# Two token groups' even projections by seven block products, attention's division moved to the gates, and its streams reordered

## The chip, the cores and the metric

One core of a Trainium2 chip runs the whole kernel. The metric is the device time of one execution in microseconds. TensorE (PE) multiplies, VectorE (DVE), ScalarE (ACT) and GpSimd (POOL) work on tiles, and all DMA is issued from the queue of SyncE (SP).

## The reference

Two sequences (2048 and 512 tokens, width 1024) go through two layers with the same weights. All is float32.

```python
def even_sublayer(x, w_in, ...):
    u = x @ w_in
    qa, ka, va, za, gd, qb, kb, vb, zb = jnp.split(u, _offsets(EVEN_SPLITS), axis=-1)
    ya = gla_mixer(qa, ka, va, za, gd, ...)   # gated linear attention, both directions, 4 heads
    yb = swa_mixer(qb, kb, vb, zb, rel_bias, sink)   # |i-j| <= 128, softmax with a sink, 8 heads
    return jnp.concatenate([ya, yb], axis=-1) @ w_out
...
    e = jnp.exp(s - m)
    p = e / (jnp.sum(e, -1, keepdims=True) + jnp.exp(sk - m))
    o = jnp.einsum('bnkgqs,bnskd->bnqkgd', p.astype(v.dtype), vb).reshape(Bn, L, SWA_WIDTH)
    return o * jax.nn.silu(z)
```

The odd layer is a projection to 4096, a gated convolution of width 3 and an output projection. Each layer ends in a LayerNorm of a residual sum.

## The kernel before

The 2560 tokens form five groups of 512: groups 0 to 3 are the long sequence, group 4 is the short one. A float32 factor is split into a high and a low part of TensorE's fp32r type, and a product of two factors is three passes (high by high, high by low, low by high), each a matmul of 128 x 128 by 512 columns.

The even input projection of a group has two kinds of stage. `tok` (`e1_tok`, L1025) makes what is wanted with tokens on partitions, in 336-wide products. `ch` (`e1_ch`, L1071) makes 21 tiles of 128 channels: for each, `dense_ch` (L569) runs 24 products into one PSUM bank, eight slices of the inner dimension by three passes. Tiles 0 to 3 are the keys, 4 to 7 the queries of the linear attention, 8 the keys and 9 to 12 the queries of the softmax attention, 13 to 16 and 17 to 20 their gates. Between them `decay` runs the small matmuls that make the decays.

Attention is cut in 20 chunks of 128 tokens. `gla_stream` (L1454) goes through a chunk with `inside` (L1186): seven levels of pairwise decay products on VectorE, each with small matmuls of 32 or 64 columns, and at its end the transposes and the state update; then `along` (L1402) goes forward. `swa_front` (L1510) makes scores, exponentials and their sums (`den`) and divides the tile `P` by them; `swa_back` (L1579) turns `P` by transposes, splits it and multiplies by the values; at the end it multiplies by the gate (`gb`) and stores to `mix_s`.

The order on the engines is written by a planner in the kernel. `Model` keeps a clock for each engine; dense stages run as the main thread, and `Flow.pump` (L337) steps side streams, by rank, whenever TensorE's clock passes the time at which their inputs are due. Attention is thus laid between the dense products. `Flow.until` (L346) runs side streams alone when a dense stage needs a mark that isn't there yet. Weights arrive by `fetch`, are split by ScalarE (`cook`, tile `wh`) and GpSimd (`cook_low`, tile `wl`).

In the odd layer two pairs of groups (`odd_pair`, L1944) already multiply 2 x 2 blocks with seven products of half the inner dimension: activations' differences from `prep_pair` (L909), weights' differences and splits from `pair_weights` (L1858), and VectorE sums that put the products together. A unit is seven products of 12 matmuls.

All recorded instructions have line L242, since one helper issues them; tiles tell them apart. `acc` and `ps` are PSUM banks (four each), `st` the activations' parts, `wh` and `wl` the weights' parts, `md`, `pr` and `y` working tiles; names ending in `_s` lie in HBM.

The stages stand in this order (`run`, L2103): tok4 ch4 tok3 ch3 tok2 ch2 tok1 ch1 oe4 tok0 ch0 one4 oe0 oo4 oe1 oe2 pair0 oe3 oo0 pair1 oo1 oo2 oo3, where oe and oo are output projections of the even and the odd layer and one4 is the odd layer's projection of group 4.

Of the kernel before, what the change touches and what calls it, by code (L numbers as in the profile page):

```python
# [262 lines left out]
class Flow:  # L263
# [32 lines left out]
    def flush(self, everything=False, name=None):  # L296
        now, keep = [], []
        for one in self.late:
            (now if everything or name in one[2] or (name is None and one[0] <= self.t) else keep).append(one)
        self.late = self.model.late = keep  # L300
        for one in now:
            one[1]()
# [74 lines left out]
class Trunk:  # L377
    def __init__(self, tc, nc, I, y_out, ctx):
# [23 lines left out]
        self.vb_s = dr("vb_s", (NC, 128, 256))  # L402
        self.qf_s = dr("qf_s", (NC, 128, 512))
# [10 lines left out]
        self.blocks = []  # L414
# [154 lines left out]
    def dense_ch(self, xh, xl, w=None, last=True):  # L569
# [3 lines left out]
        p = self.pd()  # L573
# [13 lines left out]
        if last:  # L587
            self.drop(wl)
        return p
# [86 lines left out]
    def setup(self):  # L676
# [9 lines left out]
        self.dtot = c.tile([128, NC, 4], F32, name="dtot")  # L686
# [47 lines left out]
    def setup_bias(self):  # L734
        nc, I, c = self.nc, self.I, self.const
        yield from self.setup_late()
        oh = self.e((32, 512), "gb", bufs=2)
        nc.sync.dma_start(oh[:], I["onehot"])
        ml = self.e((8, 512), "gb", bufs=2)
# [6 lines left out]
        line = self.e((8, 512), "pth", bufs=2)  # L746
# [4 lines left out]
        for h in range(8):  # L751
            rows = self.e((128, 512), "ptl", bufs=2)
# [5 lines left out]
        yield 6.0  # L758
        self.bias = [self.new(self.e2, (128, 4, 385), F32, "P", 4, True) for _ in range(2)]
# [35 lines left out]
    def prep(self, key, src, gates, homes=None, then=None, fix=None, deep=1, each=None):  # L795
# [10 lines left out]
        eager, homes = homes is not None, homes or self.half  # L806
# [218 lines left out]
    def e1_tok(self, g):  # L1025
# [9 lines left out]
        stores = {"gla_in": 24, "swa_in": 29, "done_sw": 33, "done_e1_": 37}  # L1035
# [35 lines left out]
    def e1_ch(self, groups, us):  # L1071
# [3 lines left out]
        if us[0] == 0:  # L1075
            if groups == (4,):
# [25 lines left out]
        def split(g, u, p):  # L1102
            sc = 1.0 if u == 8 else 0.125
            hi, lo = self.m2(dt=F32R), self.m2(dt=F32R)
# [6 lines left out]
            def store():  # L1111
                for i, o in enumerate((hi, lo)):
                    for hh in range(2):
# [4 lines left out]
                        else:  # L1118
                            nc.sync.dma_start(
                                self.qb_s[4 * g:4 * g + 4, 64 * i:64 * i + 64, 2 * (u - 9) + hh].rearrange("c p t -> p c t"),  # L1120
                                s.rearrange("p (c t) -> p c t", c=4))
                self.left[g]("swa_in")
            flow.defer(rest, hi, lo, p)

        def take(g, u, p):
            if u < 8:
# [7 lines left out]
                if u == 0:  # L1134
# [3 lines left out]
                    X = G[g] = self.new(self.yp, (128, 512), F32R, "y", 4, True)  # L1138
# [12 lines left out]
            if 1 < u < 10:  # L1151
                decay(g, (u - 2) // 4, (u - 2) % 4)

        for u in us:
# [7 lines left out]
            if u == 9:  # L1162
                self.drop(up, *(G[g] for g in groups))
                up = self.up = None
                G.clear()
        if u == 16:
            for g in groups:
                self.release("e1_%d" % g)
                flow.mark("end_e1_%d" % g)

# [8 lines left out]

    def gla_load_k(self, c):  # L1180
        K = self.e((128, 2, 512), "KK")
# [1023 lines left out]
```

## Time and profile before

| | us |
|---|---|
| median of three runs | 2368.6 (2367.55 to 2372.68) |
| profiled execution | 2370.12 |
| its span, first to last instruction | 2368.1 |
| TensorE busy | 2343.9 |
| VectorE busy | 1582.8 |
| GpSimd busy | 1418.4 |
| ScalarE busy | 1226.1 |

The profile has a page and views that group the same instructions: by engine and tile, by stretch of time, by waits, by DMA issue. TensorE's matmuls overlap, so the mean length of one is more than the time from one start to the next; the count in a stretch gives the pace. Softmax attention runs from 162.1 us (its first reciprocal of `den`) to 1261.1 us (the last store of `gb`).

### The profile page before, as it was taken

What the parts mean: (1) busy time and instruction counts of PE and PEld (TensorE: products, weight loads), DVE (VectorE), ACT (ScalarE), POOL (GpSimd) and SP (SyncE); (2) the same over time, 40 slices, a digit from 0 to 9 for tenths busy, and PEclk for the clock granted to TensorE, in tenths of its full rate; (3) what the DMA queues carried; (4) which work ended last, traced back from release to release, by engine and by line L of the source; (5) the groups of instructions that cost most, each with busy time, mean ns of one, the idle gap of its engine ahead of it and who ended that gap; (6) DMA issues with size and microseconds to landing.
All of it is one profiled execution on the core that took longest, in us unless ns stands there. A gap on an engine that the chain in (4) does not pass through costs nothing.

```text
span 2368.1 us, 43087 instructions
## 1 busy us (share of the span) xinstructions
PE 2343.9 (99%) x15830; PEld 1951.8 (82%) x15830; DVE 1582.8 (67%) x2699; ACT 1226.1 (52%) x2363; POOL 1418.4 (60%) x1610
## 2 busy tenths in 40 slices
PE   8999999999999999999999999999999999999998
PEld 8888889888988888888888888878888877888887
DVE  2267756767767677577776467876566587656567
ACT  4666776656576645665577532543334343333431
POOL 5454435443444444444444467898887689988674
PEclk9999999999999999999999999999999999999999
DMA  7977686676667657675478777232124633221573
GB/s 230 295 226 233 221 269 229 209 221 221 218 194 236 223 173 242 197 218 161 158 245 268 266 261 243 92 116 89 52 78 140 217 105 103 73 72 58 175 242 121
DMA packets 275057, 437.37 MB, mean 185 GB/s; under 512 B 21360, under 2 KB 160240, under 8 KB 274848
## 3 DMA queue, kind: packets, MB, share of 16 engines
q1 hardware_dynamic: 274848, 434.64, 56.5%
q8 instruction: 125, 2.05, 0.4%
q14 instruction: 84, 0.69, 0.1%
HBM read 319.72 MB, written 114.84 MB: 184 GB/s over the span
## 4 chain that ended last, share of the span: by engine, by line
PE 87%; DVE 5%; POOL 4%; DMA 2%; issue 1%; ACT 1%; SPq 0%; POOLq 0%; DVEq 0%; ACTq 0%
PE acc L242 71%; PE ps L242 17%; POOL wl L242 1%; POOL wh L242 1%; DVE st L242 1%; DVE bst L242 1%; DVE y L242 1%; POOL md L242 0%; SPq L242 0%; DVE QQ L242 0%; DVE P L242 0%; DVE KK L242 0%; DMA K<-kb_s 0%; DMA mix_s<-gb 0%; DMA op_s<-QQ 0%
## 5 line engine op out<-in xcount | busy, mean ns | idle before, releaser
L242 POOL TENSOR_TENSOR wl<-ws,wh 128x256 fp32r<-128x256 f32 (+1 forms) x912 | 750.7, 855 | 711.4 <-PE acc L242 478.0
L242 PE MATMUL acc<-st,wh 128*128 128x512 f32 x3160 | 828.5, 395 | 2.8 <-DVE pr L242 2.0
L242 PEld LDWEIGHTS acc<-st,wh 128*128 128x128 f32 x3160 | 580.9, 188 | 121.0 <-issue 3.1
L242 PE MATMUL acc<-st,wl 128*128 128x512 f32 x1744 | 471.9, 395 | 2.8 <-POOL wl L242 1.9
L242 PE MATMUL acc<-wh,st 128*128 128x512 f32 (+1 forms) x1680 | 389.4, 371 | 7.9 <-ACT st L242 6.4
L242 PEld LDWEIGHTS acc<-st,wl 128*128 128x128 f32 x1744 | 320.8, 188 | 68.0 <-POOL wl L242 4.1
L242 PEld LDWEIGHTS acc<-wh,st 128*128 128x128 f32 x1680 | 300.2, 189 | 55.1 <-ACT st L242 6.4
L242 ACT CAST wh<-ws 128x1024 fp32r<-128x1024 f32 (+2 forms) x252 | 249.0, 989 | 184.2 <-DMA ws<-in_w_oo 55.9
L242 PE MATMUL acc<-wl,st 128*128 128x512 f32 (+1 forms) x840 | 209.0, 368 | 0.6 <-POOL wl L242 0.5
L242 ACT ACTIVATE md<-md 128x512 f32<-128x512 f32 x264 | 164.7, 631 | 20.5 <-DVE md L242 14.9
L242 PEld LDWEIGHTS acc<-wl,st 128*128 128x128 f32 x840 | 150.7, 188 | 23.8 <-POOL wl L242 1.3
L242 DVE SCALAR_TENSOR_TENSOR md<-acc,md 128x512 f32<-128x512 f32 (+1 forms) x113 | 77.0, 683 | 81.5 <-ACT md L242 76.5
L242 DVE TENSOR_TENSOR st<-pr,st 128x512 fp32r<-128x512 f32 x115 | 98.5, 874 | 41.6 <-ACT st L242 41.2
L242 ACT ACTIVATE md<-acc 128x512 f32<-128x512 f32 (+1 forms) x133 | 76.2, 597 | 67.0 <-PE acc L242 66.5
L242 POOL TENSOR_TENSOR wh<-md,wh 128x256 fp32r<-128x256 f32 x118 | 96.7, 842 | 13.6 <-ACT wh L242 13.1
L242 ACT CAST pth<-ps 128x512 fp32r<-128x512 f32 x112 | 65.3, 583 | 73.1 <-PE ps L242 72.3
L242 DVE CUSTOM_DVE_ANT_0 P<-ps,P 128x384 f32<-128x384 f32 (+1 forms) x160 | 79.3, 525 | 29.6 <-PE ps L242 29.0
L242 ACT ACTIVATE P<-P,nm 128x385 f32<-128x385 f32 (+1 forms) x160 | 93.2, 587 | 3.9 <-DVE nm L242 3.9
L242 ACT ACTIVATE mv<-mv,eps 128x1 f32<-128x1 f32 x40 | 11.8, 295 | 151.8 <-DVE mv L242 147.7
L242 PE MATMUL acc<-P,wh 128*128 128x512 f32 x312 | 89.5, 400 | 0.4 <-POOL wh L242 0.4
L242 ACT COPY km<-KK 128x512 f32<-128x512 f32 x80 | 50.8, 635 | 72.2 <-DVE KK L242 50.9
L242 ACT CAST st<-pr 128x512 fp32r<-128x512 f32 x115 | 68.3, 617 | 30.3 <-DMA pr<-mix_s 12.9
(490 smaller groups left out, 4090.2 us busy)
## 6 DMA issues: line engine op xcount, KB each, us to landing
ws<-in_w_ch SPq DMA_DIRECT2D x105, 512.0 KB, 4.4
ws<-in_w_od SPq DMA_DIRECT2D x58, 512.0 KB, 4.2
ws<-in_w_oe SPq DMA_DIRECT2D x40, 512.0 KB, 3.8
ws<-in_w_oo SPq DMA_DIRECT2D x36, 512.0 KB, 3.5
K<-kb_s SPq DMA_DIRECT2D x32, 384.0 KB, 6.3
d_s<-md SPq DMA_DIRECT2D x40, 256.0 KB, 4.2
qb_s<-md SPq DMA_DIRECT2D x80, 128.0 KB, 3.9
tA<-d_s SPq DMA_DIRECT2D x20, 512.0 KB, 5.7
```

Of the source, the lines that this page charges most:

```text
L242: r = f(*a, **k)
```

## The change

**Even pair.** Groups 4 and 3 are projected together. The stages become tok4, tok3, one `ch` stage for both in which tile 0 is done plainly for each group, and then ten units (`even_pair`, new) of two channel tiles each by seven products of half the inner dimension. `prep_even` (new) makes the activations' differences on VectorE from the parts `st` that lie on chip, and puts their splits in the tiles that attention uses later (P, Q, K0, K1, V, pth, ptl, gb). `pair_weights` now serves these units too and writes two of its sums in place. Softmax attention's bias tiles are loaded after the units, when P is free.

```diff
+        even = [(1, 2), (3, 4), (5, 6), (7, 8), (13, 14), (15, 16), (9, 10), (11, 12), (17, 18), (19, 20)]
-        stages = [("tok", 4), ("ch", ((4,), A + B)), ("tok", 3), ("ch", ((3,), A + B)),
+        stages = [("tok", 4), ("tok", 3), ("ch", ((4, 3), [0], even)),
...
+        for k in range(4):
...
+            b11, b12, b21, b22 = raws
+            t = self.take(places, (128, 512))
+            sub(t[:], b12[:], b11[:])
+            sub(b12[:], b22[:], b12[:])
+            sub(b22[:], b22[:], t[:])
+            sub(b21[:], b21[:], b22[:])
...
+            for i in (1, 6, 7, 5, 2, 4, 3) if n else (1, 2, 6, 7, 5, 4, 3):
+                if n == 0 and i in (4, 5, 6, 7):
+                    yield "paire_%d" % i
...
+                p = u[i] = self.pd(hold=True)
+                for k in range(4):
+                    c = slice(k * 128, k * 128 + 128)
+                    nc.tensor.matmul(p[:], w[:, 0, c], H[i][k], start=(k == 0), stop=False)
+                    nc.tensor.matmul(p[:], w[:, 0, c], L[i][k], start=False, stop=False)
+                    yield
+                for k in range(4):
+                    c = slice(k * 128, k * 128 + 128)
+                    nc.tensor.matmul(p[:], w[:, 1, c], H[i][k], start=False, stop=(k == 3))
...
+        for i in (6, 7, 5):
+            yield "free_paire_%d" % i
```

**Division at the gates.** The four divisions of a half-block's P on VectorE go. The reciprocals are stored to a new HBM array `rd_s`, element by element, read back once per chunk as rows repeated over 64 partitions, and multiplied into the gate on GpSimd.

```diff
-                for h in range(4):
-                    nc.vector.tensor_scalar(Pt[:, h, :w], Pt[:, h, :w], den[:, h:h + 1], None, op0=ALU.mult)
...
+                    nc.sync.dma_start(self.rd_s[c, kv].rearrange("h t -> t h"), den[:])
+                    if kv:
+                        self.flow.mark("rd_%d" % c, max(0.0, self.model.clock["sync"] - self.flow.t) + 10.0)
...
+                            nc.sync.dma_start(rb[64 * i:64 * i + 64], bass.AP(a.tensor, a.offset + (2 * c + i) * 512, [[0, 64], [1, 512]]))
...
+            nc.gpsimd.tensor_tensor(flat, flat, rb[:], op=ALU.mult)
```

**Streams.** `inside` ends after its seven levels; what followed is `behind`, run by a stream of its own, `gla_behind`, gated by a mark per chunk, while `gla_stream` starts the next chunk (two chunks open at most). Level 2 now copies Q apart, as level 8 did. In `swa_back` the transposes of the next block are issued before the split of the last is done, where a PSUM bank is free. Softmax attention's streams move from rank 2 to rank 1. `flush` runs each deferred step once even if a step runs others.

```diff
+    def gla_behind(self):
+        nxt = []
+        for c in [*range(19, 15, -1), *range(15, -1, -1)]:
+            yield "head_%d" % c
...
-        flow.add(self.swa_front())
-        flow.add(self.swa_back())
+        flow.add(self.gla_behind(), rank=1)
+        flow.add(self.swa_front(), rank=1)
+        flow.add(self.swa_back(), rank=1)
```

How the instructions move, at three places. TensorE before, in the channel stage of group 4: each tile is 16 passes by `wh` and 8 by `wl`, and the first small products of linear attention (tiles `qn`, `QQ`, `KK`) stand between them.

```order
L242 MATMUL acc<-st,wh 128x512 x16
L242 MATMUL acc<-st,wl 128x512 x8
L242 MATMUL acc<-st,wh 128x512 x14
L242 MATMUL ps<-qn,KK 32x32 x16
L242 MATMUL ps<-QQ,KK 32x32 x16
L242 MATMUL acc<-st,wh 128x512 x2
```

TensorE in the change, inside a unit: two products of 12 on `st` alone and on the differences in P, Q and gb, with a level of linear attention between.

```order
L242 MATMUL acc<-st,wh 128x512 x12
L242 MATMUL ps<-md,km 32x32 x16
L242 MATMUL ps<-QQ,km 32x32 x16
L242 MATMUL acc<-st,wl 128x512 x12
L242 MATMUL acc<-P,wh 128x512 x4
L242 MATMUL acc<-Q,wh 128x512 x2
L242 MATMUL acc<-gb,wh 128x512 x2
```

What moved: a tile pair takes 84 products for two groups instead of 96, and attention's small products now stand in the units. Next, VectorE in softmax attention before: the reciprocal is followed by four divisions, ahead of a gate's step (`md`) and a level of linear attention.

```order
L242 TENSOR_TENSOR ptl<-ps,pth 128x512
L242 RECIPROCAL den<-den 128x4
L242 TENSOR_SCALAR P<-P,den 128x384 x4
L242 SCALAR_TENSOR_TENSOR md<-acc,md 128x512
L242 TENSOR_TENSOR QQ<-QQ,tC 128x64x2x4
```

In the change the next step follows the reciprocal at once, and splits of two turned blocks (`ptl`) stand together.

```order
L242 TENSOR_TENSOR ptl<-ps,pth 128x512 x2
L242 RECIPROCAL den<-den 128x4
L242 TENSOR_TENSOR gb<-ps,gb 64x512
L242 TENSOR_TENSOR ptl<-ps,pth 128x512 x2
L242 ISA P,mx<-ps,P 128x384
```

What moved: the divisions left VectorE's queue. SP before, where softmax attention loads its gate (`gb`) among the weight tiles and the stores of the projections:

```order
L242 DMA mix_s<-gb 512x1x128
L242 DMA gb<-gb_s 128x512
L242 DMA ws<-in_w_ch 128x1024
L242 DMA qb_s<-md 64x4x128 x4
L242 DMA qf_s<-QQ 128x512
```

SP in the change, around the second read-back: other transfers, the read-back in two halves, the write of the next half-block's reciprocals, and the next weight tile behind them.

```order
L242 DMA vb_s<-md 128x256
L242 DMA pr<-in_xT 128x512
L242 DMA md<-rd_s 64x512 x2
L242 DMA k_s<-md 128x4x128
L242 DMA rd_s<-den 128x4x1
L242 DMA ws<-in_w_ch 128x1024
```

What moved: the `rd_s` rows are new, and weight tiles stand behind them; SP has 1304 DMA issues before and 1360 now.

More of the change, by code (lines that the diff above doesn't have):

```diff
@@ L296, in flush @@
     def flush(self, everything=False, name=None):
[L297 to L300, printed above, removed]
+        now = [one for one in self.late if everything or name in one[2] or (name is None and one[0] <= self.t)]
         for one in now:
-            one[1]()
+            if any(one is x for x in self.late):
+                self.late[:] = [x for x in self.late if x is not one]
+                one[1]()
     def force(self, *tiles):
@@ L793, in let_go, with prep @@
                 self.drop(t)
-    def prep(self, key, src, gates, homes=None, then=None, fix=None, deep=1, each=None):
+    def prep(self, key, src, gates, homes=None, then=None, fix=None, deep=1, each=None, wide=False):
         nc = self.nc
@@ L804, in prep @@
         raws = []
-        eager, homes = homes is not None, homes or self.half
+        eager, homes = homes is not None, homes or self.half + (self.mids if wide else [])
         todo = list(range(8))
@@ L1161, in e1_ch @@
                 yield
-            if u == 9:
+            if u == 7 and not units:
                 self.drop(up, *(G[g] for g in groups))
@@ L1165, in e1_ch @@
                 G.clear()
+        if units:
+            own = self.owned["e1_%d" % groups[1]]
+            self.drop(*own[:2])
+            del own[:2]
+            flow.mark("plain_e")
+            yield from self.even_pair(groups, units, take, put, decay)
         if u == 16:
@@ L1178, in gla_load, with gla_home @@
         return q, T1
+    def gla_home(self, tag):
+        done = self.flow.done
+        rows = "swa_in1" in done and "res_x1_4_3" not in done
+        return [(self.e2, tag, 1)] if rows or self.model.spare(tag, 1) else self.large[:1]
     def gla_load_k(self, c):
-        K = self.e((128, 2, 512), "KK")
+        K = self.take(self.gla_home("KK"), (128, 2, 512))
         for i in range(2):
@@ L1232, in inside @@
         base = None
-        Sb = self.bst if not last else None
         wait = []
@@ L1452, in seq, with ahead @@
         return (0, 16) if g < 4 else (16, 20)
+    def gla_behind(self):
+        nxt = []
+        for c in [*range(19, 15, -1), *range(15, -1, -1)]:
+            yield "head_%d" % c
+            v = nxt.pop() if nxt else self.load_v(c)
+            def ahead():
+                if c not in (0, 16) and "gla_in%d" % ((c - 1) // 4) in self.flow.done:
+                    nxt.append(self.load_v(c - 1))
+            yield from self.behind(*self.heads.pop(0), v, ahead)
+            v = None
     def gla_stream(self):
+        nxt = {}
```

424 lines of the change are left out of this document (332 added, 92 removed).

## The prediction

> **What bounds the kernel now.** I read the spans first, then the page's busy shares, the chain that ended last, what TensorE waited for, and then stretches of the run, because the run has two kinds of work.
>
> ```profile
> core 0: 2368.1 us, clock 0.998
> PE 2343.9 (99%) x15830; PEld 1951.8 (82%) x15830; DVE 1582.8 (67%) x2699; ACT 1226.1 (52%) x2363; POOL 1418.4 (60%) x1610
> PE 87%; DVE 5%; POOL 4%; DMA 2%; issue 1%; ACT 1%; SPq 0%; POOLq 0%; DVEq 0%; ACTq 0%
> L242 PEld LDWEIGHTS acc<-st,wh 128*128 128x128 f32 x3160 | 580.9, 188 | 121.0 <-issue 3.1
> ```
>
> The clock is full (0.998), TensorE is busy for 99% of the span, and 87% of the chain is TensorE's own time. A busy TensorE may still be one that starts products slowly, so I looked at stretches. The columns are the stretch, its length, then busy time and instructions of TensorE, weight loads, VectorE, ScalarE, GpSimd, then clock, DMA share and GB/s.
>
> ```profile
> 59.20:118.40 59.20, 59.20 (x263) 49.03 (x262) 12.48 (x18) 36.20 (x56) 27.43 (x39) 1.00 0.97 295
> 473.60:532.80 59.20, 59.20 (x634) 48.51 (x633) 40.74 (x82) 34.42 (x62) 26.88 (x30) 1.00 0.75 221
> 1065.60:1124.80 59.20, 58.89 (x560) 47.88 (x559) 47.01 (x102) 35.38 (x70) 27.28 (x31) 1.00 0.51 161
> 1480.00:1539.20 59.20, 58.27 (x278) 47.54 (x277) 49.84 (x64) 31.00 (x57) 48.70 (x46) 1.00 0.29 92
> 1539.20:1598.40 59.20, 57.13 (x242) 46.06 (x241) 45.22 (x54) 23.91 (x38) 57.23 (x55) 0.97 0.33 116
> 1657.60:1716.80 59.20, 59.20 (x260) 48.52 (x259) 34.15 (x43) 23.30 (x33) 48.22 (x50) 1.00 0.15 52
> 1894.40:1953.60 59.20, 57.20 (x263) 46.17 (x262) 52.72 (x65) 26.13 (x50) 51.92 (x48) 1.00 0.31 105
> 1953.60:2012.80 59.20, 57.64 (x250) 46.55 (x250) 45.29 (x51) 23.61 (x39) 55.67 (x54) 1.00 0.30 103
> ```
>
> The stretch from 1657.6 holds nothing but 512-wide products: 260 in 59.20 us, one every 0.2277 us. That is my price of a dense product. From 59.2 to 118.4, where group 4 runs its channel projections alone, TensorE goes at the same pace, with VectorE only 21% busy. In the stretches with attention between the dense products (473.6, 1065.6) TensorE still has next to no idle time. The idle time that there is lies at the starts of the two seven-product stages of the odd layer.
>
> ```profile
> PE acc L242 <- ACT st L242: 6.4, 1, 6.4
> PE acc L242 <- POOL wl L242: 2.4, 3, 1.1
> PE acc L242 <- DVE pr L242: 2.0, 2, 1.3
> ```
>
> In the table of TensorE's waits (us in total, times, longest) the largest is the one at the program's start. So the run is as long as TensorE's list of work, and a shorter list shortens it unless a new wait fills the hole.
>
> By the Trainium skill's page "Perfetto Trace Analysis", section "Identifying the Most-Contended Engine", matmul busy time is a poor measure of headroom and the busy share of weight loads is a better one; here that share is 82%, which would leave 18%. By that rule the removed work would be 120 weight loads of 0.188 us (the last row above), an estimate of 22.6 us instead of the 27.3 below. The trace speaks for the product count: in the stretch from 1657.6, which cannot go faster, the weight loads are also at 48.52 of 59.20 us, 82%.
>
> **Seven products for eight.** Twenty of 21 channel tiles of groups 4 and 3 go from 10 x 2 x 2 x 24 = 960 products to 10 x 7 x 12 = 840; every other kind of TensorE instruction keeps its count. All are 512 wide, so the list is 120 x 0.2277 = 27.3 us shorter. The weight pieces change too: 40 tiles of 1024 columns become 70 of 512.
>
> ```profile
> L242 POOL TENSOR_TENSOR wl<-ws,wh 128x256 fp32r<-128x256 f32 x852 | 712.2, 868 | 677.2 <-PE acc L242 467.0 <-ACT wh L242 137.9 <-PE ps L242 12.4
> L242 POOL TENSOR_TENSOR md<-ws,md 128x512 f32<-128x512 f32 x9 | 11.7, 1297 | 0.0
> L242 DVE TENSOR_TENSOR md<-acc,md 128x512 f32<-128x512 f32 x91 | 61.1, 681 | 13.4 <-PE acc L242 11.3 <-ACT md L242 1.3
> L242 DVE TENSOR_TENSOR st<-pr,st 128x512 fp32r<-128x512 f32 x115 | 98.5, 874 | 41.6 <-ACT st L242 41.2
> ```
>
> (After the count: busy us, mean ns of one, then idle time before and what ended it.) A unit of seven products lasts 84 x 0.2277 = 19.1 us. GpSimd makes 14 low halves of 0.868 us in it, 12.2 us, and up to four weight sums of 1.297 us, 5.2 us: 17.4 us in all, under the 19.1. In the stretch from 1657.6 it carries 48.22 of 59.20 us in the same pattern with no idle TensorE, so I cost it at nothing; if that cover failed, each us over 19.1 would cost ten, one per unit. The DMA load halves per unit of time (two tiles per 19.1 us instead of one per 24 x 0.2277 = 5.5 us).
>
> VectorE adds 7 sums of 0.681 us per unit, 4.8 us. The differences of the activations are 48 instructions of 128x512 between 0.681 and 0.874 us, 33 to 42 us in all, and most of them fall in the first 70 us, where the stretch from 59.2 shows that VectorE has room. But the last must be done before the first unit's third product. The nearest rows are the starts of the odd pairs, where parts are also made and products wait for them: 0.93 + 2.07 us of idle TensorE and a clock of 0.97 from 1480 to 1598, and 2.00 + 1.56 us from 1894 to 2013, so 3.6 to about 4.8 us (the 0.03 of clock is 1.8 us). The added start could be hidden (0) or be both of these in a row (8.4). I take 6, since the tok part of group 3 now runs in the same 30 us and needs VectorE for its own results.
>
> The clock belongs to that price:
>
> ```profile
> 1549.60 0.73 PE L242 MATMUL acc<-st,wl 128*128 128x512 f32 x2 [1.14 <-POOL wl L242]
> 1551.27 1.08 PE L242 MATMUL acc<-st,wl 128*128 128x512 f32 x2 [0.94 <-DVE acc L242]
> ```
>
> Two waits of 1.14 and 0.94 us stand 1.7 us apart in the one odd-layer stretch whose clock fell to 0.97, so waits of this size bunched at a start may cost nearly twice their length. The Trainium skill's page "TensorE: Matmul & The Clock Gate", section "The HAM clock gate", has the clock halve only after an idle window of about 3.4 us; the trace does not agree, as no wait in that stretch is that long.
>
> **Attention in less time.** The softmax attention can start only when the units are done, since its tiles hold the differences: counted over the order with the prices of the trace, some 275 us into TensorE's list instead of some 140. Both kinds of attention still end in the first part of oe0. Softmax attention so has some 17% less time; linear attention starts as early as before. VectorE loses the divisions.
>
> ```profile
> L242 DVE TENSOR_SCALAR P<-P,den 128x384 f32<-128x384 f32 x128 | 61.6, 543 | 1.1
> L242 DVE TENSOR_SCALAR P<-P,den 128x256 f32<-128x256 f32 x32 | 10.9, 405 | 0.3
> L242 POOL TENSOR_TENSOR gb<-gb 128x512 f32<-128x512 f32 x20 | 27.3, 1367 | 61.4 <-DVE gb L242 61.4
> ```
>
> That is 61.6 + 10.9 = 72.5 us of busy time less on VectorE, and 20 more gate products of 1.367 us, 27.3 us, on GpSimd, which is 45% busy in those stretches (26.88 of 59.20). Neither is TensorE's time, so the direct gain is nothing. VectorE's share per stretch stays about what it is: 40.7 to 47.0 us of 59.2 in the rows above, for both kinds together in some 10% less time, less 72.5 us over some 950 us (8%). The waits it could add are bounded below by 0 and above by what the busiest VectorE stretch shows (52.72 of 59.20 busy, 2.00 us of idle TensorE): over 950 us that is 16 x 2.0 = 32 us. I take 5, near the row at 1065.6, where VectorE has 47.01 and TensorE lost 0.31 us; 16 x 0.31 = 5.0.
>
> **Fewer changes of work.** The two streams and overlapped turns put attention in larger pieces: counted over the order, attention and other small work stands between dense products in 486 places before and in 384 now. What a change costs stands in the timeline (start, us, engine):
>
> ```profile
> 641.81 0.34 PE L242 MATMUL ps<-qn,KK 128*32 128x32 f32 x20
> 641.97 0.56 PE L242 MATMUL ps<-QQ,KK 128*32 128x32 f32 x32
> 642.46 0.50 PE L242 MATMUL ps<-pth,V 128*128 128x512 f32 x1
> 642.80 0.40 PE L242 MATMUL ps<-ptl,V 128*128 128x512 f32 x1
> 643.03 0.85 PE L242 MATMUL acc<-st,wl 128*128 128x512 f32 x3
> ```
>
> The first wide product after small ones holds the next back by 0.34 us where the one after takes 0.23. At 0.11 us each, 102 places less are 11 us. Since larger pieces also have changes inside them, the gain could be 0, and with the slow step into the first wide one (0.49 us for 32 small products, where the 20 before them take 0.16 us, so some 0.23 more) up to 102 x 0.34 = 35 us; I take 9, near the 0.11.
>
> **The denominators' trip.** Each of the 40 half-blocks writes 512 values of 4 bytes to HBM and 20 read-backs in two halves follow, on SP's one queue.
>
> ```profile
> SPq L242 <- POOL wl L242: 490.1, 195, 7.4
> qb_s<-md SPq DMA_DIRECT2D x80, 128.0 KB, 3.9
> gb<-gb_s SPq DMA_DIRECT2D x20, 256.0 KB, 5.0
> ```
>
> SP waits for other engines most of the time, and a read-back is held until 10 us after its write was queued. The nearest write in small pieces (512 bytes) lands in 3.9 us. So SP should not stand, and the gate product that needs it is late in nobody's way: 0. If a write took longer than the 10 us, SP would stand with the next weight tiles behind it, and TensorE would feel it once the two tiles in hand, 2 x 5.5 us, were used up. The Trainium skill's page "DMA: Bandwidth & Descriptors", section "Specifications", speaks against this edit: below 512 bytes the DMA engines read, modify and write. No row here shows a write of 4-byte pieces to HBM by data, so this stays a rival.
>
> **The sum.** Against the profiled execution (2370.12 us, span 2368.1): -27.3 products, -9 changes of work, +6 start of the units, +5 denser attention, 0 for weights, gates and denominators: -25.3, so 2344.8. The median of the runs, 2368.6, is 1.5 lower: 2343.3, rounded to **2343 us**.
>
> **Rivals.**
> 1. The bank returns bind in the units. Each product holds a PSUM bank until VectorE has added it; beside the 4.8 us of sums VectorE has gates, decays and the linear attention of group 4. Speaking for it: VectorE at 49.84 and 52.72 of 59.20 where the odd pairs lose time. Against: 34.15 in the steady part. If every unit lost the 2.0 us that the whole stretch from 1894.4 lost, 10 x 2.0 = 20 us come on top: 2363. Chance 0.12.
> 2. Slower than before: the trip of the denominators stops SP. Place: the 20 read-backs. It decides from the point where a write needs over 10 + 11 = 21 us to land; at 24 us each costs 3 us, 60 us in all, 2343 + 60 = 2403. Speaking for it: 512 single pieces; against: 3.9 us for the nearest write and a queue that is slack. Chance 0.06; other ways to a slower run (a unit's weights late by more than 3.5 us ten times) 0.02.
> 3. The change moves TensorE's waits but not its end: the shorter list meets a denser attention with the full 32 us of waits, -27.3 - 9 + 6 + 32 = +1.7: 2370. Chance 0.06.
> My forecast keeps 0.74.
>
> **Range and chances.** The low end has both gains and no start cost at the larger price of a change of work between 0.11 and 0.34: 2368.6 - 27.3 - 11 = 2330. The high end takes in rival 1 with a little over: 2364. A difference of 0.2% (4.7 us) is about what a measurement of this kernel can tell, so "same" is 2363.9 to 2373.3: rival 3 and the upper edge of rival 1, 0.07. Slower 0.08, faster 0.85.
>
> **What would show it.** Right: 120 fewer 512-wide products, and TensorE still at 99%; the stretch from about 75 to 290 us with under 8 us of idle TensorE; the last attention product some 20 us earlier than now; no wait of SP on rd_s over 3 us. Wrong: waits of TensorE on VectorE sums in every unit (rival 1), SP waiting for DMA rd_s with weight tiles late (rival 2), or idle pieces spread over 300 to 1250 us (rival 3). The stages from oo4 on should take the same time to within 1 us each.

## The result, and the profile after

The changed kernel takes 2497.94 us (median of 4 runs, 2493.8 to 2504.49), the kernel before 2369.36 us (2367.55 to 2372.68) beside it: a ratio of 1.0542, 95% interval 1.0527 to 1.0557. It is 5.4% slower where I had forecast 1.1% faster; the time lies far outside the range.

The span and clock of the changed kernel:

```profile
core 0: 2491.7 us, clock 0.978
```

Its busy times, and the number and size of the DMA packets:

```profile
PE 2359.8 (95%) x15710; PEld 1957.2 (79%) x15710; DVE 1641.8 (66%) x2675; ACT 1244.7 (50%) x2430; POOL 1479.8 (59%) x1628
...
DMA packets 295923, 431.18 MB, mean 173 GB/s; under 512 B 42736, under 2 KB 181104, under 8 KB 295712
```

The 120 products are gone (15830 to 15710). The DMA engines move some 20900 packets more than before (275057), of which 40 x 512 = 20480 are the pieces of the denominators. And TensorE, 24.2 us idle in the span before, is idle for 2491.7 - 2359.8 = 131.9 us, and its shorter list keeps it busy for 15.9 us longer, at a clock of 0.978 in place of 0.998. In stretches (length, then busy time and instructions of TensorE, weight loads, VectorE, ScalarE, GpSimd, then clock, DMA share, GB/s), first of the kernel before: its last 956.6 us, the stretch in which the units now stand, and the one of its attention:

```profile
1411.50:2368.10 956.60, 941.01 (x4161) 769.93 (x4159) 656.24 (x803) 366.66 (x578) 764.57 (x778) 1.00 0.37 124
75.00:290.00 215.00, 215.00 (x1967) 181.26 (x1966) 131.74 (x274) 138.06 (x253) 105.16 (x137) 1.00 0.76 239
147.00:1221.00 1074.00, 1072.14 (x9928) 903.94 (x9917) 766.40 (x1641) 672.64 (x1374) 471.96 (x594) 1.00 0.67 213
```

and then of the changed kernel: the last 956.6 us, the stretch of the units, and the one in which softmax attention runs:

```profile
1535.10:2491.70 956.60, 941.29 (x4164) 769.58 (x4163) 658.04 (x804) 366.81 (x578) 763.77 (x778) 1.00 0.37 125
75.00:290.00 215.00, 206.16 (x1509) 166.40 (x1507) 160.12 (x223) 131.73 (x233) 146.34 (x151) 0.98 0.58 177
340.00:1440.00 1100.00, 1013.37 (x8825) 847.29 (x8813) 680.11 (x1442) 642.32 (x1431) 436.90 (x539) 0.96 0.83 205
```

The end of the program is the same within 0.3 us of work. The units lose 8.84 us where nothing was lost before. Most of the loss is in the third row of the changed kernel: 86.6 us idle, and a clock of 0.96. What TensorE waits for is no one thing (whole run; us in total, times, longest; 5.9 of the 13.6 us for QQ lie in the units):

```profile
PE ps L242 <- DVE QQ L242: 13.6, 9, 5.3
PE acc L242 <- ACT wh L242: 13.2, 2, 11.9
PE ps L242 <- DMA V<-vb_s: 12.2, 3, 8.2
PE ps L242 <- DVE ptl L242: 10.6, 11, 6.9
```

Linear attention, weight tiles, the values and the splits of softmax attention are late, each a few times. What they share shows in the timeline (start, us, engine; behind a row the idle time before it and what ended it), at the first of these writes and again 137 us later:

```profile
355.46 0.39 SPq L242 DMA_DIRECT2D rd_s<-den  x1
355.90 0.56 SPq L242 DMA_DIRECT2D V<-vb_s  x1
...
368.71 0.76 PE L242 MATMUL ps<-pth,V 128*128 128x512 f32 x1 [8.21 <-DMA V<-vb_s]
...
491.66 0.35 SPq L242 DMA_DIRECT2D ws<-in_w_ch  x1
492.42 0.37 SPq L242 DMA_DIRECT2D rd_s<-den  x1
493.09 0.33 SPq L242 DMA_DIRECT2D ws<-in_w_ch  x1
...
502.65 1.04 ACT L242 CAST wh<-ws 128x1024 fp32r<-128x1024 f32 x1 [19.83 <-DMA ws<-in_w_ch]
...
503.74 1.22 PE L242 MATMUL acc<-st,wh 128*128 128x512 f32 x2 [11.88 <-ACT wh L242]
```

At the first place SP does not stand: it issues the load of V 0.44 us after the write. But V is there only 12.8 us after its issue, where such a load takes 4.7 us in the kernel before, and a weight tile issued at 491.66 is there at 502.65, 11.0 us later for 4.4:

```profile
ws<-in_w_ch SPq DMA_DIRECT2D x105, 512.0 KB, 4.4
...
V<-vb_s SPq DMA_DIRECT2D x16, 384.0 KB, 4.7
```

From 360 to 365 us the DMA engines move 17 GB/s all together, where the mean of the run is 173. The second place is less clean: SP itself had stood for 6.5 us up to 482.35, until a store issued 6 us after another of these writes had landed, and the weight tile has ahead of it all the transfers that SP then issued in a row. So the transfers around a write of the denominators are late, whoever they are for.

Three theories stood against each other. A: the 40 writes of 512 pieces of 4 bytes hold up the packets beside them. B: attention squeezed into less time binds on VectorE. C: the read-back makes SP's queue stand (rival 2). After the first four runs a fourth theory came for what was left of the loss, D: the even pair has a price of its own, at its start and where VectorE is full in the units.

### The profile page after: what moved, and what is told of

Same layout as the page of the kernel before. It is cut to its first block, busy times and chain, and to the rows that moved or that the text cites. A ratio compares the mean times of both kernels' runs of the same rounds, so it can differ in the third digit from the quotient of the medians.

```text
span 2491.7 us, 43037 instructions
## 1 busy us (share of the span) xinstructions
PE 2359.8 (95%) x15710; PEld 1957.2 (79%) x15710; DVE 1641.8 (66%) x2675; ACT 1244.7 (50%) x2430; POOL 1479.8 (59%) x1628
## 5 line engine op out<-in xcount | busy, mean ns | idle before, releaser
L242 POOL TENSOR_TENSOR wl<-ws,wh 128x256 fp32r<-128x256 f32 (+1 forms) x760 | 625.6, 855 | 680.8 <-PE acc L242 258.6
L242 PE MATMUL acc<-st,wh 128*128 128x512 f32 x2756 | 731.7, 399 | 14.5 <-ACT wh L242 11.9
L242 PEld LDWEIGHTS acc<-st,wh 128*128 128x128 f32 x2756 | 513.4, 190 | 119.5 <-ACT wh L242 12.3
L242 PE MATMUL acc<-st,wl 128*128 128x512 f32 x1572 | 424.0, 397 | 3.2 <-POOL wl L242 1.2
L242 ACT CAST wh<-ws 128x1024 fp32r<-128x1024 f32 (+2 forms) x226 | 215.8, 955 | 246.1 <-DMA ws<-in_w_ch 69.6
L242 ACT ACTIVATE md<-md 128x512 f32<-128x512 f32 (+1 forms) x287 | 179.4, 631 | 31.2 <-DVE md L242 21.8
L242 POOL TENSOR_TENSOR wh<-y,wh 128x256 fp32r<-128x256 f32 x106 | 105.2, 1012 | 29.3 <-ACT wh L242 29.3
L242 PE MATMUL acc<-P,wh 128*128 128x512 f32 x414 | 118.4, 397 | 0.4 <-POOL wh L242 0.4
L242 ACT CAST pth<-ps 128x512 fp32r<-128x512 f32 x112 | 62.9, 584 | 73.4 <-PE ps L242 67.5
L242 DVE TENSOR_TENSOR md<-acc,md 128x512 f32<-128x512 f32 (+1 forms) x126 | 77.2, 620 | 28.8 <-PE acc L242 13.7
L242 PEld LDWEIGHTS acc<-P,wh 128*128 128x128 f32 x414 | 77.5, 188 | 20.0 <-POOL wh L242 2.1
```

What stands on the lines that cost most here:

```text
L242: r = f(*a, **k)
```

## The experiments

### The division back, or the denominators in rows

The changed kernel with the division put back on VectorE, so that nothing goes through HBM:

```diff
-                    nc.sync.dma_start(self.rd_s[c, kv].rearrange("h t -> t h"), den[:])
...
+                for h in range(4):
+                    nc.vector.tensor_scalar(Pt[:, h, :w], Pt[:, h, :w], den[:, h:h + 1], None, op0=ALU.mult)
...
-            nc.gpsimd.tensor_tensor(flat, flat, rb[:], op=ALU.mult)
```

> The changed kernel with the four divisions of P back on VectorE and without the reciprocals' trip through HBM; all else stays. Theory A (the 40 writes of 512 single 4-byte pieces hold up the DMA packets behind them, so inputs and weights come late): the loss after the units goes, about 130 us, 2350 to 2380 us. Theory B (attention squeezed in less time binds on VectorE): VectorE gets 72 us more to do, 2500 to 2530 us. Theory C (the read-back stops SP's queue): as A, 2350 to 2380 us.

And with trip and gates kept, but the denominators turned by TensorE and written as 4 rows of 512 bytes:

```diff
-                    nc.sync.dma_start(self.rd_s[c, kv].rearrange("h t -> t h"), den[:])
+                nc.tensor.transpose(pr[:4, :128], den[:], self.ident[:])
...
+                nc.scalar.copy(dr[:4, :128], pr[:4, :128])
...
+                    nc.sync.dma_start(self.rd_s[c, kv], dr[:4, :128])
```

> The changed kernel with the division still at the gates and the trip through HBM kept, but the reciprocals are turned by TensorE first (40 transposes, 40 small copies), so that each write is 4 rows of 512 bytes instead of 512 pieces of 4 bytes. Theory A: 2345 to 2380 us. Theory B: about 2498 us, no change. Theory C: the trip and its waits are still there, about 2498 us.

Measured: 2396.05 us (ratio to before 1.0111, 1.0096 to 1.0126) and 2388.11 us (1.0076, 1.0061 to 1.0091). Either takes over 100 us of the loss away, the second with the trip and the read-back kept. Both lie above the ranges that theory A gave them (up to 2380), and neither gets under the kernel before. In both the planner has ordered the instructions anew.

### The writes alone, in the kernel before

Two kernels add only 40 writes of 2 KB to the kernel before, which nobody reads: of the denominators in 512 pieces of 4 bytes, and of P in 4 rows of 512 bytes.

```diff
+                self.flow.defer(lambda c=c, kv=kv, den=den: nc.sync.dma_start(
+                    self.rd_s[c, kv].rearrange("h t -> t h"), den[:]), den)
```

> The kernel before with nothing but the 40 writes of the reciprocals in 4-byte pieces added; nobody reads them. Theory A: the writes alone cost some 3 us each, 2440 to 2510 us. Theories B and C: nothing to wait for, 2365 to 2380 us.

```diff
+                self.flow.defer(lambda c=c, kv=kv, Pt=Pt: nc.sync.dma_start(
+                    self.rd_s[c, kv], Pt[:4, 0, :128]), Pt)
```

> The kernel before with 40 writes of the same 2 KB at the same places, but as 4 rows of 512 bytes (values of P, read by nobody). Theory A: 2365 to 2380 us, since the pieces are long. If 40 more DMA issues on SP's queue were enough to do the harm: as the run with 4-byte pieces.

Measured: 2535.51 us (1.0693, 1.066 to 1.0726) and 2369.75 us (1.0001, 0.9991 to 1.001) beside 2369.59 us. The small pieces cost 165.9 us, 4.1 us a write, and the same bytes in rows nothing. The order of the instructions on the compute engines is that of the kernel before. That is theory A, and it ends theory C, since no read-back exists here. TensorE's waits in the kernel with 4-byte pieces show how little their names tell:

```profile
PE ps L242 <- DVE QQ L242: 54.5, 18, 8.6
```

In the kernel before the same two engines have these waits for VectorE:

```profile
PE acc L242 <- DVE st L242: 0.2, 1, 0.2
PE ps L242 <- DVE QQ L242: 0.2, 1, 0.2
```

The 54.5 us read as if VectorE had become slow. It has the same instructions as before and is busy for less time (1560.8 us for 1582.8); what is new ahead of it is only the writes.

### The change in its own order, without small pieces

This one has the order of the changed kernel on every engine.

```diff
-                    nc.sync.dma_start(self.rd_s[c, kv].rearrange("h t -> t h"), den[:])
+                    nc.sync.dma_start(self.rd_s[c, kv], Pt[:4, 0, :128])
```

> The changed kernel in its own order on every engine, the 40 writes at their places in SP's queue, of 2 KB as before; only that each write takes 4 rows of 512 bytes of P where the changed kernel takes 512 values of 4 bytes of the denominators, so the gates are multiplied by values of P and the output is not the reference's. If the small pieces are what costs (theory A), nearly all that the changed kernel lost to its version with rows of 512 bytes goes: that one took 2388.1 us with 40 transposes and copies more, some 4 us of TensorE, so about 2384, and no packets of over 1.5 us are left. If the waits come from the arrangement, the two streams and the later attention, with VectorE's full stretches (theory B), most of the 128 us stay: over 2440. What is left over before's 2369.6 in the first case, about 15 us where the forecast had 25 us less than before, is then the price of the new arrangement alone.

Measured: 2374.03 us, 1.0018 (1.0009 to 1.0027). So the small pieces cost 2497.94 - 2374.03 = 124 us, nearly the whole loss of 128.6, and 10 us more of it than expected. Its span, then its busy times, then the stretch of the units and the one that lost 86.6 us:

```profile
core 0: 2372.0 us, clock 0.996
```

```profile
PE 2322.1 (98%) x15710; PEld 1936.7 (82%) x15710; DVE 1642.1 (69%) x2675; ACT 1244.8 (52%) x2430; POOL 1486.8 (63%) x1628
```

```profile
75.00:290.00 215.00, 205.28 (x1550) 165.89 (x1549) 161.49 (x228) 131.84 (x234) 148.23 (x153) 1.00 0.58 179
340.00:1440.00 1100.00, 1087.82 (x9271) 918.17 (x9272) 753.64 (x1530) 686.31 (x1517) 514.18 (x617) 1.00 0.71 230
```

In the second row idle time falls from 86.6 to 12.2 us and the clock is full. Over the span the pieces cost 119.7 us: 131.9 - 49.9 = 82.0 of idle time and 2359.8 - 2322.1 = 37.7 in which the same list ran slower at the lower clock. The units' loss (first row, 9.72 us) is untouched: it is another matter.

The packets in the trace show whom the small pieces hold up. In the changed kernel 899 packets took over 1.5 us, the longest 8.9, and 802 of them ended within 12 us after one of the 40 writes was issued. With rows there are 33 such packets, the longest 2.3 us, and in the kernel before 48, the longest 2.7. (None had been expected to be left.) The packets of 4 bytes themselves took 9 ns in the median: it is the large ones beside them that stand.

And the change without its small pieces is no gain: 1.0018 lies at the edge of what can be told from no change, on the slow side.

A further version made one transpose and one write of 8 rows out of two of 4:

```diff
+                    nc.tensor.transpose(pr[:8, :128], both[:], self.ident[:])
...
+                        nc.sync.dma_start(self.rd_s[c].rearrange("k h t -> (k h) t"), dr[:8, :128])
```

> The changed kernel with the denominators of both half-blocks of a chunk turned by TensorE in one transpose and written as 8 rows of 512 bytes: 20 transposes, copies and writes where the version with 4 rows has 40. By theory A nothing is left to gain on the transfers, only half of the transposes: 2384 to 2388, still slower than before. If the number of writes costs too, 2375 or less.

Measured: 2382.14 us, 1.0043 (1.0031 to 1.0056), 2 us under the range for the case that nothing is left to gain on the transfers, and far from the 2375 of the other. The planner's order is another here too; that 40 row writes cost nothing stands on the run in the kernel before (2369.75).

### What in a write of small pieces costs

Four more kernels before, each with 40 unread writes. They differ only in the destination and the columns taken.

```diff
...
+                    self.rd_s[c, kv].rearrange("h (a t) -> (h a) t", t=4), den[:]), den)
```

> The kernel before with 40 writes more of the denominators, as 128 pieces of 16 bytes each, which nobody reads. 512 pieces of 4 bytes cost 166 us in all (4.1 us a write), 4 rows of 512 bytes nothing. If the price goes by the number of pieces, a quarter of 166 us is left: 2411. If it goes by the bytes, or by any write below 512 bytes alike, it stays near 2535. If it needs pieces of 4 bytes, it is gone: 2370.

```diff
...
+                    self.rd_s[c, kv, 0:1].rearrange("h t -> t h"), den[:, 0:1]), den)
```

> The kernel before with 40 unread writes of 128 pieces of 4 bytes each: as many pieces as in the write that cost nothing (128 of 16 bytes), as small as in the one that cost 4.1 us (512 of 4 bytes). If a piece of 4 bytes costs by itself, a quarter of 166 us: 2411. If the price needs 512 pieces in one write, nothing: 2370.

```diff
...
+                    self.rd_s[c, kv, 0:2].rearrange("h (a t) -> (h a) t", t=2), den[:, 0:2]), den)
```

> The kernel before with 40 unread writes of 128 pieces of 8 bytes, one behind the other in HBM. Pieces of 4 bytes cost 107.6 us here, pieces of 16 bytes nothing. If the price falls with the size of a piece, something between: some 50 us, 2420. If it hangs on pieces of 4 bytes alone, nothing: 2370. If every piece below 16 bytes costs alike, 2475.

```diff
+        self.rd_s = dr("rd_s", (NC, 2, 128, 128))
...
+                    self.rd_s[c, kv, :, 0:1], den[:, 0:1]), den)
```

> The kernel before with 40 unread writes of 128 pieces of 4 bytes, each piece 512 bytes from the next in HBM instead of side by side; the same order on every engine as with the pieces side by side, which took 2476.65. If the price comes from neighbours, pieces of several DMA engines in one stretch of 512 bytes, it goes: 2370. If a piece of 4 bytes costs by itself wherever it lands, it stays: about 2475.

| a write | us | ratio to before (95%) | us a write |
|---|---|---|---|
| 512 pieces of 4 B, side by side | 2535.51 | 1.0693 (1.066 to 1.0726) | 4.1 |
| 128 pieces of 4 B, side by side | 2476.65 | 1.0459 (1.0444 to 1.0475) | 2.7 |
| 128 pieces of 8 B, side by side | 2374.28 | 1.0026 (1.0015 to 1.0038) | 0.14 |
| 128 pieces of 16 B, side by side | 2369.95 | 0.9994 (0.9985 to 1.0003) | 0 |
| 128 pieces of 4 B, 512 B apart | 2369.05 | 1.0003 (0.9994 to 1.0013) | 0 |
| 4 rows of 512 B | 2369.75 | 1.0001 (0.9991 to 1.001) | 0 |

Two of my expectations fell. The price does not go by the number of pieces: a quarter of them cost not a quarter but 65%. And a piece of 4 bytes costs nothing by itself: the fifth row has the same instructions in the same order as the second, and only the place in HBM where the pieces land is other. The price belongs to pieces of 4 bytes that land side by side. The packets agree: over 1.5 us took 999 with the pieces side by side, the longest 8.6 us, and 62 with the pieces apart, the longest 2.2. How long the write itself takes from issue to landing goes along, pieces of 4 bytes side by side first, then 16 bytes, then 4 bytes apart:

```profile
DMA to landing us min/median/max: 8.2/9.1/10.0
```

```profile
DMA to landing us min/median/max: 1.4/3.6/9.3
```

```profile
DMA to landing us min/median/max: 1.4/3.0/6.7
```

In the first of these three kernels a load of V takes 10.5 us to land, in the second 5.5:

```profile
V<-vb_s SPq DMA_DIRECT2D x16, 384.0 KB, 10.5
```

```profile
V<-vb_s SPq DMA_DIRECT2D x16, 384.0 KB, 5.5
```

Why neighbours of 4 bytes are so slow, and of 16 not, these runs don't show.

### The whole change with pieces of 16 bytes, in its own order

Pieces of 16 bytes give a version of the change that leaves nothing out and keeps its order: the four denominators of a query stay side by side, and the gate's product reads them with a stride.

```diff
-                    nc.sync.dma_start(self.rd_s[c, kv].rearrange("h t -> t h"), den[:])
+                    nc.sync.dma_start(self.rd_s[c, kv].rearrange("h (a t) -> (h a) t", t=4), den[:])
...
-            nc.gpsimd.tensor_tensor(flat, flat, rb[:], op=ALU.mult)
+            nc.gpsimd.tensor_tensor(gb[:], gb[:], rb[:].rearrange("p (t h) -> p h t", h=4), op=ALU.mult)
```

> The changed kernel in its own order on every engine, with one thing else: the denominators are written with the four of a query side by side, 128 pieces of 16 bytes a write, and the gate's product reads them with a stride of 16 bytes. The result is the reference's. Theory A: pieces of 16 bytes cost nothing (before with them took 2369.95), so the time of the changed kernel with rows of 512 bytes, 2374, give or take 3; only if GpSimd's strided product holds the gates up is it more, at most 20 products of some 1.4 us, 2402. Then the whole loss of the change is the size of its pieces, and what is left of it is no gain.

Measured: 2376.16 us, 1.003 (1.0019 to 1.0041): as expected. The other layout of the denominators takes 122 us from the change; GpSimd's strided product is 1.578 us for 1.339.

### Why that is still no gain: VectorE in the units

In the same order, VectorE's work in the units is cut down.

```diff
-        add = lambda o, x, y: nc.vector.tensor_tensor(o[:], x[:], y[:], op=ALU.add)
+                nc.vector.engine.tensor_tensor(o[:, :128], x[:, :128], y[:, :128], op=ALU.add)
...
+            n = 1 if s == 1 else max(1, 64 // s)
+            nc.vector.engine.tensor_tensor(x[:, :n], x[:, :n], y[:, :n], op=ALU.mult)
```

> The kernel with pieces of 16 bytes, in the same order on every engine, with less work on VectorE where the units of the even pair run: the three sums of a unit that are made in place take 128 of 512 columns, and the doubling products of group 4's linear attention a quarter or less of theirs, so the output is not the reference's. VectorE was 27 of 30 us busy there, and falls to some 20. If VectorE is what TensorE waits for in the units (theory D), the waits between 190 and 300 us go, about 11 us: 2363. If they are for something else (the planned order, weights, banks that ScalarE returns), no more than 3 us: 2371 or more.

Measured: 2366.91 us, 0.9989 (0.9977 to 1.0), 9.3 us under the version it is cut from, between the two cases and nearer the first. Stretches of the units, first in that version, then with less VectorE work:

```profile
180.00:210.00 30.00, 27.45 (x302) 21.56 (x301) 26.97 (x37) 18.86 (x32) 22.29 (x21) 1.00 0.49 167
210.00:240.00 30.00, 28.40 (x247) 22.72 (x251) 27.35 (x39) 19.43 (x35) 23.04 (x22) 1.00 0.54 167
240.00:270.00 30.00, 25.39 (x351) 20.47 (x349) 26.77 (x43) 11.49 (x21) 17.35 (x17) 1.00 0.58 155
```

```profile
180.00:210.00 30.00, 30.00 (x354) 23.71 (x353) 25.86 (x44) 22.70 (x40) 21.66 (x23) 1.00 0.46 153
210.00:240.00 30.00, 29.90 (x261) 24.18 (x260) 27.49 (x43) 18.76 (x34) 22.11 (x23) 1.00 0.66 193
240.00:270.00 30.00, 29.12 (x370) 23.43 (x369) 19.95 (x42) 10.99 (x20) 14.83 (x16) 1.00 0.75 219
```

TensorE's 8.8 us of idle time in these 90 us fall to 1.0. VectorE is still 25.86 and 27.49 of 30 us busy in the first two rows, as the work comes sooner: it is the work per unit that shrank. The waits, again of the version it is cut from and then of it:

```profile
PE acc L242 <- DVE st L242: 8.1, 4, 3.4
PE acc L242 <- ACT st L242: 7.8, 3, 5.9
PE ps L242 <- DVE QQ L242: 6.3, 7, 1.7
PE acc L242 <- ACT wh L242: 3.8, 1, 3.8
...
PE ps L242 <- DVE mx L242: 3.0, 4, 1.1
...
PE ps L242 <- DVE ptl L242: 1.5, 3, 0.6
```

```profile
PE acc L242 <- DVE st L242: 7.2, 4, 3.4
...
PE ps L242 <- DVE QQ L242: 0.2, 1, 0.2
```

The waits for QQ, the queries of linear attention, are the units' price. The run cuts both the sums and the doubling products, which make QQ itself, so it doesn't tell which of the two holds QQ up. Those for `st`, the parts of the next stage's tokens, are not, so one more kernel cut the differences before the units too:

```diff
+            for o, x, y in ((b12, b22, b12), (b22, b22, t), (b21, b21, b22)):
+                nc.vector.engine.tensor_tensor(o[:, :128], x[:, :128], y[:, :128], op=ALU.subtract)
```

> The kernel with VectorE's work in the units cut down (2366.91), in the same order on every engine; as well, the differences of group 3's and 4's parts that are made in place before the units take 128 of 512 columns, 12 products of about 1.05 us to a quarter, so the output is not the reference's. If TensorE's wait of 3.5 us at 54 us, with the half clock behind it, comes from VectorE too (theory D), it goes: about 2362. If it is group 3's loads or the planned order, 2366 to 2368.

Measured: 2364.54 us, 0.9978 (0.9968 to 0.9987). The interval meets that of the kernel without the cut, so the time does not decide it. In the trace the wait at 54 us, 3.4 us long in the row above, is shorter, but there (between 40 and 90 us):

```profile
PE acc L242 <- DVE st L242: 2.0, 1, 2.0
```

VectorE has a share in it; the rest stays open.

### Versions meant to pay

Two kernels, each the 16-byte version with one more edit, give VectorE's work in the units to other engines: the last sum of a unit to ScalarE and GpSimd, and the doubling of group 4's keys to GpSimd.

```diff
-                add(u["u1"], u[3], u["u1"])
+                nc.scalar.copy(t[:], u[3][:])
+                nc.gpsimd.tensor_tensor(u["u1"][:], t[:], u["u1"][:], op=ALU.add)
```

> The kernel with pieces of 16 bytes; in each unit the last of VectorE's seven sums is made by ScalarE (copy out of the bank) and GpSimd (the sum). The planner orders the work anew. The result is the reference's. By theory D VectorE loses ten sums of 0.68 us out of some 110 us in the stretch, which is too little to end its waits: 2 to 4 us, 2370 to 2372, less than the planner's other order can move the time either way (some 10 us). If it takes 2364 or less, VectorE's saturation is a narrow one and the change could be made to pay.

```diff
-            nc.vector.tensor_tensor(kk, kk, total(s, n + 1, -n - 1), op=ALU.mult)
+            (nc.gpsimd if c >= 16 else nc.vector).tensor_tensor(kk, kk, total(s, n + 1, -n - 1), op=ALU.mult)
```

> The kernel with pieces of 16 bytes, with the doubling products of the keys of group 4's linear attention (KK by the decays, some 4 us a chunk on VectorE where the units run) on GpSimd, which is 20 of 30 us busy there. The planner orders the work anew; the result is the reference's. If the relief of VectorE is what counts (theory D: VectorE's cut in the units gave 9.3 us), some 5 us under the 2376 of the version in its own order, about 2371, no better than before; it beats both kernels only under 2364. If GpSimd, which also makes the units' weights, becomes the next thing waited for, or the new order costs more than it gains (summing on GpSimd did: 2382.6), 2376 or more.

Measured: 2382.56 us (1.0052, 1.0039 to 1.0064) and 2381.46 us (1.0043, 1.0029 to 1.0057). Neither pays. The first is 10 us over what was expected of it; the second came out as the last case said, 2376 or more. It does relieve the units, from 25.39 to 28.55 us of TensorE in this stretch (from 111.0 to 115.0 of the 120 us from 180 on):

```profile
240.00:270.00 30.00, 28.55 (x367) 23.03 (x366) 28.05 (x39) 11.06 (x20) 23.52 (x21) 1.00 0.61 168
```

but the planner's new order has TensorE wait for the parts of later stages, 17.4 us where the version it comes from has 8.1:

```profile
PE acc L242 <- DVE st L242: 17.4, 4, 8.5
```

Last, the gates' division alone, in rows, in the kernel before:

```diff
-                for h in range(4):
-                    nc.vector.tensor_scalar(Pt[:, h, :w], Pt[:, h, :w], den[:, h:h + 1], None, op0=ALU.mult)
...
+                nc.tensor.transpose(pr[:4, :128], den[:], self.ident[:])
...
+            nc.gpsimd.tensor_tensor(flat, flat, rb[:], op=ALU.mult)
```

> The kernel before with one part of the change alone, the division at the gates, with the denominators turned by TensorE and written as 4 rows of 512 bytes; no pair of even groups, no second stream. It takes 160 divisions (72.5 us net) from VectorE and adds 40 small transposes, some 4 us of TensorE, 20 products on GpSimd. If VectorE is not what binds beside the attention (theory D: the rest of the loss is the even pair's), it takes what before takes or up to 6 us more: 2369 to 2376. If VectorE binds there (theory B), it is faster by 10 us or more: under 2360. If the trip itself costs even in rows, through the gates that come later, over 2380.

Measured: 2394.26 us, 1.0093 (1.0078 to 1.0109): slower than either theory had it.

```profile
PE 2353.5 (98%) x15870; PEld 1952.7 (82%) x15870; DVE 1515.1 (63%) x2537; ACT 1232.3 (51%) x2403; POOL 1438.9 (60%) x1632
```

VectorE is 67.7 us less busy than before and TensorE, with a span of 2393.2 us, 39.7 us idle where it had been 24.2. So 67.7 us taken from VectorE bought nothing here. Its time lies where the third case of the expectation stood, but what TensorE waits for is not the gates:

```profile
PE acc L242 <- ACT st L242: 8.5, 2, 6.0
PE acc L242 <- DVE st L242: 5.1, 2, 4.9
PE acc L242 <- ACT wh L242: 3.9, 3, 2.7
```

These are parts and weights of later stages (of the 8.5 us, 6.0 are the program's start, where the kernel before has 6.4). Whether the 24 us are the gates' price or that of the planner's new order can't be told from this kernel; that is left open.

No version that computes everything was faster than the kernel before. No run has the even pair alone or the new streams alone, so what each of them is worth is not shown.

## Why the prediction was wrong

**The denominators' trip, priced at 0: this step failed.** I took the nearest row, 512-byte pieces that land in 3.9 us, as near enough for pieces of 4 bytes side by side, and asked only what SP would do. The small pieces of the trip cost 119.7 us of span (124 in the medians), on the same order of work. The rival that had the sign, rival 2, had another mechanism: SP standing before read-backs, from a landing of 21 us on. SP did wait there a little:

```profile
SPq L242 <- DMA rd_s<-den: 25.7, 10, 4.8
```

But the kernel with 4-byte writes that nobody reads has the same wait, 24.1 us in 10 times, and loses more, and pieces that land within 10.0 us cost 2.7 us a write. So both signs that I had set for rival 2 showed, SP's wait on `rd_s` and late weight tiles, and its mechanism was still not the cause. What is late are the transfers beside a write, so the place is the whole of 340 to 1440 us, not the 20 read-backs. The clock adds to it: 37.7 of the 119.7 us are not waits but products that run slowly beside them (a clock of 0.978 for 0.996), and I had priced that for the start alone. I had read only the threshold of 512 bytes. The Trainium skill's page "DMA: Bandwidth & Descriptors" has another rule, in its section "Rules for kernel authors": a last dimension that is strided is lowered to one descriptor per element, and should be rearranged to be contiguous. That speaks against just this write, and the runs agree in part, with 4.1 us a write for the strided pattern and nothing for 16 bytes in a row; but 128 single elements cost 2.7 us a write side by side and nothing 512 bytes apart, so the elements alone are not the price.

**Seven products for eight, -27.3: right in its count.** 120 products fewer. TensorE's busy time in the same-order kernel is 2322.1, 21.8 us less than before; the clock of 0.996 in place of 0.998 takes some 4.8 us of the 27.3 back (0.004 x 2372.0 less 0.002 x 2368.1), and 0.7 are left over. By the Trainium skill's rule that weight loads are the better measure (page "Perfetto Trace Analysis", section "Identifying the Most-Contended Engine") I had estimated 22.6 us. The weight loads fell by 15.1, from 1951.8 to 1936.7, and the time by neither figure.

**Fewer changes of work, -9: not there.** The sum just made leaves no room for it: TensorE's busy time holds the slow starts, and it fell by the products and no more. Added up over the trace, the starts that come 50 to 200 ns later than is usual after a product of that width are 64.8 us before and 62.9 in the same-order kernel. Larger pieces have their changes inside them; I had named that as the case of 0.

**The start of the units, +6: about right. Waits inside them, 0: wrong.** At the start TensorE waits 3.4 us for `st` at 54 us, and the clock is 0.93 from 40 to 88 us, another 0.07 x 48 = 3.4 us (same-order kernel; in the 16-byte version it is 0.96 and 1.9 us):

```profile
40.00:88.00 48.00, 44.63 (x247) 41.06 (x245) 44.70 (x62) 20.09 (x40) 39.49 (x41) 0.93 0.56 180
```

The work cut from VectorE in the units was worth 9.3 us, for which the sum had no term; `st` by VectorE has two more waits, of 2.4 and 2.0 us, at later stages. Rival 1 had VectorE as the engine that binds, and it is nearly full, at 27 of 30 us; but the waits are, by their names, for linear attention's queries and not for the banks, and the price is half of the 20 us that it had. I had compared VectorE's share in the odd pairs' steady part, 34.15 of 59.20, where no attention runs beside.

**Denser attention, +5: about right.** In the same-order version with 16-byte pieces TensorE waits 3.0 us for `mx` and 1.5 for `ptl`. The stretch as a whole loses more, 12.2 us in the same-order kernel where 1.9 had been lost, part of it to weights and to parts of later stages. Rival 3, a full 32 us, did not come.

**Weights, 0, and the later stages: nearly right.** TensorE waits 13.2 us for `wh` only while the small pieces run, 3.8 without them and 0.8 before; the last 956.6 us are the same. But "the last attention product some 20 us earlier" was wrong by far: the last product on `ptl` and V starts at 1256.3 us before and at 1351.7 in the same-order kernel (first and last start in each row, kernel before and then same order):

```profile
L242 PE MATMUL ps<-ptl,V x112: 387/395/503, 195.4 to 1256.3; 128*128 128x512 f32 x112
```

```profile
L242 PE MATMUL ps<-ptl,V x112: 387/392/499, 358.9 to 1351.7; 128*128 128x512 f32 x112
```

By these rows softmax attention starts 163.5 us later, where I had counted 135, and ends 95.4 later. There is room for that in this order, and the time doesn't show it.

The sum, by spans: forecast -25.3. Measured without small pieces +3.9: -27.3 of products, +25.7 of idle time, +5.5 of clock and rest. The small pieces add 119.7 to that. (The low end of the range speaks of the larger price of a change of work, but its 11 us are 102 x 0.11, the smaller one; the result lies far from that end.)

## What to carry to other kernels

Before an array goes to HBM in another order than it has on chip, look at what lands next to what: keep 16 bytes or more of a partition together, or turn the tile first, and undo the order when it is read on chip; here that was worth 122 us. If no row of the profile shows a transfer of that shape, add it unread to the kernel before and time it, since its price can fall on the transfers beside it, as here, and not on the transfer itself. And when the list of the busiest engine gets shorter, look in that stretch for the engine that follows; here VectorE was busy for 27 of 30 us.

## What the runs showed of the hardware

Writes of neighbouring 4-byte pieces from 128 partitions to HBM hold up other transfers (single packets took up to 8.6 us with 512 bytes a write, and 11.0 with 2 KB) and cost this program 2.7 us a write for 512 bytes and 4.1 us for 2 KB; with pieces of 8 bytes it is 0.14 us, with 16 bytes or with 512 bytes from piece to piece nothing that can be measured. The Trainium skill's page "DMA: Bandwidth & Descriptors", section "Specifications", has the engines read, modify and write below 512 bytes. The runs agree that small writes can be dear, but all five small kinds lie below 512 bytes and only neighbours of 4 bytes cost much: size alone is not the price.
